# A hybrid HGRN2 and retention layer: bursts ordered by tile shape, copies first in a tree's level, bounds and tables inside the opening

## The chip, the core and the metric

The kernel runs on one core of a Trainium2 chip. The core has a matmul engine (PE, with its weight loads shown as PEld), a vector engine (DVE), a scalar engine (ACT), a general engine (POOL), and SP, whose queue issues most of the DMAs. Each engine takes its own instructions in a fixed order and waits on semaphores for the others. The metric is the device time of one execution in microseconds (us); lower is better.

## The reference

The layer takes x (2048 positions of 1024 features) and a condition c. What is computed, in one pass:

```python
mod = silu(c) @ w_ada + b_ada                   # shift, scale, gate
h = rms_norm(x, norm_g) * (1 + scale) + shift
hq, hf, hi, hz, rq, rk, rv, rz, ga, gb = split(h @ w_in)
f = lb + (1 - lb) * sigmoid(hf); k = 1 - f; q = silu(hq)   # lb from hg_lb_logits, a softmax
S_t = diag(f_t) S_{t-1} + k_t hi_t^T;  oA_t = S_t^T q_t    # HGRN2, 8 heads of 128
oB = retention(rotary(rq), rotary(rk), rv)                 # 8 heads, dk 64, dv 128, causal decay
uA = head_rms_norm(oA) * silu(hz); uB = head_rms_norm(oB) * silu(rz)
m = sigmoid(ga) * uA + sigmoid(gb) * uB
out = rms_norm(x + gate * (m @ w_out), final_g)
```

## The kernel before, in words

**Products.** The projection h @ w_in is done in two halves of 1024 positions. Its columns are cut into "quads" of kinds a (HGRN2 q and f of a head), b (retention q and k), v (the two value streams) and A, B (gates), in the order of the table `ORDER`. Each quad is a 2 by 2 block product done with seven products instead of eight (a Strassen form): product m = 1 to 7 of quad q multiplies a left operand (the parts A11, A12, A22 of h, or the sums S1 to S4 of them) by a right operand (a weight part or a sum of weight parts) and adds into one PSUM bank, tag v, x or y. Every operand is split into a rounded high part and a remainder, and `product_step` issues three 128x512 matmuls for each of the 4 steps along the contraction: 12 matmuls for a product. ACT makes the high part (L295) and DVE the remainder (L296). Product 2 takes A12 (in the trace simply A) and a weight as it is, with no sum on either side; products 5, 3 and 6 take S1 to S4. `product_order` (L55) lists the sequence of (m, quad).

**The end of a product.** `after` (L486) evicts a bank by ACT (L483, `stash`) or adds it by DVE (L496, L503, L507) and hands the block to `deliver`, which starts what follows for it: sigmoid, f, k and q for kind a (`take_a`, L580 to L590), a transposition for v (`take_v`, L597).

**Background.** Everything else is cut into steps that stand between the products. `Background.burst` (L201) is called about every 8 matmul steps and runs one step of each generator in its one list `lanes`. A head's `tree` and `hgrn_out` are appended to that list; a pair's `retention` is put at its front. So a burst's order is retention, then the tree and the output of each head as they were appended. PE takes its instructions in the order in which the program gives them; the order on the other engines is laid out by a scheduler from priorities (`FIRSTS` = 2000, `PEV` = 600, else 0).

**The tree.** For each head and half, the products of decays within a chunk are built in levels m = 1, 2, 4, 8, 16, 32, 64. Level m makes 64 small matmuls (128 deep, 32 or fewer wide; from m = 16 on fewer and larger ones) into a bank of tag lv, of which there is one. Then DVE multiplies q (L787), k (L788), below m = 16 also every 16th column k0 (L791), and f (L792) for the next level, and copies the level's result out of the bank through masks into `ad` (L794 for the diagonal, L799); from m = 16 on ACT copies it into `af` (L812, L818). The next level's matmuls need the new q and k, and the bank.

**HGRN2 output and retention.** A step of `hgrn_out` makes three matmul pairs into poh. A retention step transposes a key block, makes the scores (64 deep, tile rt), adds the cross term from the state rs (64 deep) and scm times v (128 deep) into pos, and the state's update kz times v (64 wide). Both end in `normed` (L833): ACT sums squares (L838), POOL makes the power (L174, L177), ACT scales (L841).

**The opening** (L1108 to L1247) has no sums of h yet. It builds h by 8 feature blocks in the order KO while DVE reduces two weight rows of w_ada for each (L355, read by `ada_load` through SP), and adds quad 0 with plain products into the banks c00, c10, c11 (tag x0) and c01, and products 1 and 2 of quad 1 beside them (x1, y1; c_y in the trace is the tile that holds c01 and y1). Behind its loop stand `lower_bounds` (L159 to L169, an exponential on ACT), the four deliveries of quad 0, `late_consts` and `tables` (L614), which reads the cosine and sine tables, transposes them on DVE (L618) and stores them to DRAM (lin) with 12 DMAs from SP.

## Time and profile before

| what | value |
|---|---|
| time, median of 3 runs | 2061.95 us (2058.75 to 2062.59) |
| time of the profiled execution | 2059.39 us |
| its span from the first to the last instruction | 2057.6 us |
| mean granted clock of PE | 0.988 |
| PE busy | 1950.7 us, 95% of the span |
| DVE, ACT, POOL busy | 1413.2, 984.9, 284.5 us |
| DMA | 126 GB/s on average |

A row of the timeline gives the start and the length of a merged group of equal instructions, its engine and line, out<-in by the program's names, how many, and in brackets how long the engine was idle before it and which instruction ended that. Lengths of matmuls are modelled and overlap the next ones; the distance between two starts is the better measure. 128\*32 is the tile of the array that a matmul takes.

### The profile page before, as it was taken

What the parts mean: (1) busy time and instruction counts of PE and PEld (TensorE: products, weight loads), DVE (VectorE), ACT (ScalarE), POOL (GpSimd) and SP (SyncE); (2) the same over time, 40 slices, a digit from 0 to 9 for tenths busy, and PEclk for the clock granted to TensorE, in tenths of its full rate; (3) what the DMA queues carried; (4) which work ended last, traced back from release to release, by engine and by line L of the source; (5) the groups of instructions that cost most, each with busy time, mean ns of one, the idle gap of its engine ahead of it and who ended that gap; (6) DMA issues with size and microseconds to landing.
All of it is one profiled execution on the core that took longest, in us unless ns stands there. A gap on an engine that the chain in (4) does not pass through costs nothing. (4 is left out here: it accounts for less than half of the span.)

```text
span 2057.6 us, 40131 instructions
## 1 busy us (share of the span) xinstructions
PE 1950.7 (95%) x15172; PEld 1581.2 (77%) x15172; DVE 1413.2 (69%) x2677; ACT 984.9 (48%) x2426; POOL 284.5 (14%) x522
## 2 busy tenths in 40 slices
PE   4889899998999989999999999998999999999998
PEld 3668688877778777777787788877788878787887
DVE  5885767666767767677987676676757675768332
ACT  4634444554555446445544545544454445445331
POOL 2002210121013210201002020211011101110000
PEclk9999999999999999999999999999999999999999
DMA  9144424343353545446544424354434433245542
GB/s 305 43 106 122 129 78 115 101 133 114 113 159 113 138 133 157 144 149 201 153 104 128 121 79 109 100 147 127 115 100 123 122 84 114 69 128 189 160 147 83
DMA packets 453122, 259.97 MB, mean 126 GB/s; under 512 B 171713, under 2 KB 406209, under 8 KB 452929
## 3 DMA queue, kind: packets, MB, share of 16 engines
q1 hardware_dynamic: 286752, 172.89, 29.5%
q10 hardware_dynamic: 153120, 76.04, 13.1%
q0 software_dynamic: 13056, 8.47, 1.6%
q8 instruction: 120, 1.97, 0.4%
q14 instruction: 74, 0.60, 0.1%
HBM read 188.03 MB, written 69.21 MB: 125 GB/s over the span
## 5 line engine op out<-in xcount | busy, mean ns | idle before, releaser
L296 DVE TENSOR_TENSOR b<-w,b 128x512 fp32r<-128x512 f32 (+1 forms) x553 | 346.7, 635 | 312.8 <-ACT b L295 304.0
L71 PE MATMUL v<-S,b 128*128 128x512 f32 x1704 | 430.8, 401 | 10.6 <-ACT S L295 5.0
L295 ACT ACTIVATE b<-w 128x512 fp32r<-128x512 f32 (+1 forms) x553 | 316.8, 583 | 256.1 <-PE x L71 169.3
L71 PE MATMUL x<-S,b 128*128 128x512 f32 x1704 | 433.3, 399 | 5.0 <-DVE c L503 4.4
L71 PE MATMUL x<-A,b 128*128 128x512 f32 x1704 | 424.6, 397 | 3.9 <-ACT c L483 3.0
L71 PEld LDWEIGHTS v<-S,b 128*128 128x128 f32 x1704 | 320.4, 192 | 82.7 <-ACT c L483 7.5
L71 PEld LDWEIGHTS x<-A,b 128*128 128x128 f32 x1704 | 317.6, 190 | 71.1 <-ACT c L483 4.2
L71 PEld LDWEIGHTS x<-S,b 128*128 128x128 f32 x1704 | 312.8, 189 | 67.6 <-ACT uh L838 3.3
L71 PE MATMUL y<-A,b 128*128 128x512 f32 x840 | 207.5, 395 | 1.8 <-DVE ro L650 1.8
L421 DVE TENSOR_TENSOR w<-w,w 128x512 f32<-128x512 f32 x284 | 195.0, 687 | 3.8 <-DMA w<-in_w_d_dram 0.3
L71 PEld LDWEIGHTS y<-A,b 128*128 128x128 f32 x840 | 155.6, 189 | 34.4 <-issue 2.2
L71 PE MATMUL ops<-wo,m 128*128 128x512 f32 x768 | 174.5, 389 | 0.0
L71 PEld LDWEIGHTS ops<-wo,m 128*128 128x128 f32 x768 | 144.1, 188 | 29.9
L174 POOL TENSOR_SCALAR ssh<-ssh 128x1 f32<-128x1 f32 x128 | 49.7, 388 | 788.8 <-ACT uh L838 785.6
L483 ACT ACTIVATE c<-v 128x512 f32<-128x512 f32 x142 | 84.5, 595 | 123.9 <-PE v L71 106.0
L841 ACT ACTIVATE uh<-poh,rrh 128x128 f32<-128x128 f32 x128 | 47.1, 368 | 137.4 <-POOL rrh L177 131.8
L71 PEld LDWEIGHTS lv<-q,k 128*32 128x32 f32 (+1 forms) x5888 | 70.1, 109 | 54.3 <-issue 39.9
L71 PE MATMUL lv<-q,k 128*32 128x16 f32 (+2 forms) x5888 | 81.4, 188 | 29.2 <-DVE ad L799 12.4
L787 DVE TENSOR_TENSOR q<-q,f 128x512 f32<-128x512 f32 x112 | 76.9, 687 | 16.8 <-PE lv L71 16.6
L177 POOL TENSOR_TENSOR rrh<-ssh,mhalf 128x1 f32<-128x1 f32 x128 | 86.3, 674 | 10.4
L503 DVE TENSOR_TENSOR c<-c,x 128x512 f32<-128x512 f32 x71 | 48.8, 687 | 53.5 <-PE x L71 53.3
L176 POOL TENSOR_TENSOR ssr<-ssr,epsx 128x2 f32<-128x2 f32 x64 | 20.5, 321 | 457.2 <-ACT ur L838 457.1
(191 smaller groups left out, 2446.9 us busy)
## 6 DMA issues: line engine op xcount, KB each, us to landing
w<-in_w_d_dram ACTq DMA_DIRECT2D x128, 256.0 KB
w<-in_w_c_dram ACTq DMA_DIRECT2D x66, 256.0 KB
mu<-ud SPq DMA_DIRECT2D x64, 256.0 KB
w<-in_w_a_dram ACTq DMA_DIRECT2D x60, 256.0 KB
wa<-in_w_ada_dram SPq DMA_DIRECT2D x16, 512.0 KB
w<-in_w_b_dram ACTq DMA_DIRECT2D x32, 256.0 KB
vd<-vt SPq DMA_DIRECT2D x128, 64.0 KB
vh<-vd SPq DMA_DIRECT2D x64, 128.0 KB
```

The costliest lines, as they stand in the source:

```text
L71: return tc.keep_in_program_order(nc.tensor.matmul(**kw))
L174: G.tensor_scalar(out=ss, in0=ss, scalar1=n * EPS, scalar2=None, op0=ALU.add)
L176: G.tensor_tensor(out=ss, in0=ss, in1=eps, op=ALU.add)
L177: G.tensor_tensor(out=dst, in0=ss, in1=mhalf.broadcast_to([P, w]), op=ALU.pow)
L295: S.activation(out=t[0], in_=src, func=AF.Copy)
L296: return V.tensor_tensor(out=t[1], in0=src, in1=t[0], op=ALU.subtract)
L421: V.tensor_tensor(out=out, in0=x, in1=y, op=ALU.add)
L483: S.activation(out=t, in_=ps, func=AF.Copy)
L503: V.tensor_tensor(out=t, in0=t, in1=xb[q], op=ALU.subtract)
L787: V.tensor_tensor(out=qv, in0=qv, in1=tv[:, :, :, 0:1].broadcast_to([P, NU, nb, m]), op=ALU.mult)
L841: S.activation(out=dsts[i], in_=pos[i], func=AF.Copy, scale=rr[:, i : i + 1])
```

## The change

1. **Order of products.** Product (2, quad 1) moves from behind (6, 1) to directly behind the opening, ahead of (5, 1), (3, 1) and (6, 1). It takes the bank that held c11, so c11 is delivered second, with priority `FIRSTS` for c11 and c10, and the opening's plain steps fill c11 and its neighbour before c10.
2. **Bounds and tables.** The load of `lg` moves up to second on SP and `lower_bounds` to the start of the opening; `tables` moves from behind the opening into its loop, at step 5 of 10.
3. **Bursts.** `lanes` is parted in three lists; a burst runs HGRN2 outputs, then retentions, then trees.
4. **Retention step.** The matmuls that are 128 deep (the transposition, scm times v) come first, then those 64 deep (cross term, scores), then the 64 wide (kz times v). The cross term closes the sum that it opened before.
5. **Tree level.** The copies out of the bank come ahead of the four multiplications.

```diff
--- before.py
+++ after.py
@@ -53,10 +53,10 @@
 
 
 def product_order():
-    made = [(5, 1), (3, 1), (6, 1)]
+    made = [(2, 2), (5, 1), (3, 1), (6, 1)]
     for i in range(1, NQ):
         n = i + 1
-        made += [(2, n), (7, i), (1, n), (5, n), (4, i), (3, n), (6, n)] if n < NQ else [(7, i), (4, i)]
+        made += [(7, 1), (1, 2), (5, 2), (4, 1), (3, 2), (6, 2)] if i == 1 else [(2, n), (7, i), (1, n), (5, n), (4, i), (3, n), (6, n)] if n < NQ else [(7, i), (4, i)]
     return made
 
 
@@ -140,13 +140,13 @@
         xrows.append(pool.tile([P, n], F32, name=f"xrow{t}", tag=tag, bufs=bufs)[:, 0:1024])
         nc.sync.dma_start(out=xrows[t], in_=a["x"][t * P : (t + 1) * P, :])
 
+    lg = upool.tile([P, 256], F32, name="lg", tag="dT", bufs=1)[:, 0 : 2 * H]
+    nc.sync.dma_start(out=lg, in_=a["lb_t"])
     ng = const("ng", [P, KT], a["ng_t"])
     bad = const("bad", [P, 2 * KT], a["bada_t"])
     for t in range(4):
         load_rows(t)
 
-    lg = upool.tile([P, 256], F32, name="lg", tag="dT", bufs=1)[:, 0 : 2 * H]
-    nc.sync.dma_start(out=lg, in_=a["lb_t"])
     lb = cpool.tile([P, H], F32, name="lb", tag="lb")
     omlb = cpool.tile([P, H], F32, name="omlb", tag="omlb")
     nomlb = cpool.tile([P, H], F32, name="nomlb", tag="nomlb")
@@ -190,6 +190,8 @@
 
         def __init__(self):
             self.lanes = []
+            self.rets = []
+            self.trees = []
             self.side = []
             self.late = []
             self.since = 0.0
@@ -200,14 +202,16 @@
 
         def burst(self):
             done = False
-            now = list(self.lanes)
+            now = self.lanes + self.rets + self.trees
             while now:
                 again = []
                 for g in now:
                     try:
                         said = next(g)
                     except StopIteration:
-                        self.lanes.remove(g)
+                        for z in (self.rets, self.trees, self.lanes):
+                            if g in z:
+                                z.remove(g)
                         done = True
                         continue
                     done = done or said is not True
@@ -258,7 +262,7 @@
 
         def drain(self):
             for _ in range(4000):
-                if not (self.lanes or self.side or self.posts):
+                if not (self.rets or self.trees or self.lanes or self.side or self.posts):
                     return
                 self.force()
             raise RuntimeError("the background does not end")
@@ -589,7 +593,7 @@
         else:
             V.tensor_tensor(out=q[:, tb * 512 : (tb + 1) * 512], in0=z, in1=sg, op=ALU.mult)
         if (ch, tb) == (0, 1):
-            bg.lanes.append(tree(h, sb, f, k, q))
+            bg.trees.append(tree(h, sb, f, k, q))
             bg.lanes.append(hgrn_out(h, sb))
 
     def take_v(sb, h, s, tb, z):
@@ -607,7 +611,7 @@
 
         bg.post(5.0, store)
         if (s, tb) == (0, 1) and h % 2:
-            bg.lanes.insert(0, retention(h // 2, sb))
+            bg.rets.insert(0, retention(h // 2, sb))
 
     lin = dram("lin", [3, 32, L])
 
@@ -784,12 +788,6 @@
             qv = q.rearrange("p (j n two m) -> p j n two m", j=NU, two=2, m=m)[:, :, :, 1, :]
             kv = kk if m >= 16 else k[:, 1 : NU * 512 + 1]
             kv = kv.rearrange("p (j n two m) -> p j n two m", j=NU, two=2, m=m)[:, :, :, 0, :]
-            V.tensor_tensor(out=qv, in0=qv, in1=tv[:, :, :, 0:1].broadcast_to([P, NU, nb, m]), op=ALU.mult)
-            V.tensor_tensor(out=kv, in0=kv, in1=tv[:, :, :, 1:2].broadcast_to([P, NU, nb, m]), op=ALU.mult)
-            if m < 16:
-                k0 = k16j[:, :, :, 0]
-                V.tensor_tensor(out=k0, in0=k0, in1=t_cur.rearrange("p j (n t) -> p j n t", n=32)[:, :, :, 1], op=ALU.mult)
-            V.tensor_tensor(out=f[:, :, 0:nb], in0=tv[:, :, :, 0], in1=tv[:, :, :, 1], op=ALU.mult)
             if m == 1:
                 V.copy_predicated(
                     out=ad.rearrange("p c (w j) -> p c w j", w=2)[:, :, :, 0], mask=dmsk,
@@ -813,6 +811,12 @@
                         out=af[r0 : r0 + m, :, r0 + m : r0 + 2 * m],
                         in_=ps[r0 : r0 + m, 0 : NC * m].rearrange("p (c t) -> p c t", t=m), func=AF.Copy,
                     )
+            V.tensor_tensor(out=qv, in0=qv, in1=tv[:, :, :, 0:1].broadcast_to([P, NU, nb, m]), op=ALU.mult)
+            V.tensor_tensor(out=kv, in0=kv, in1=tv[:, :, :, 1:2].broadcast_to([P, NU, nb, m]), op=ALU.mult)
+            if m < 16:
+                k0 = k16j[:, :, :, 0]
+                V.tensor_tensor(out=k0, in0=k0, in1=t_cur.rearrange("p j (n t) -> p j n t", n=32)[:, :, :, 1], op=ALU.mult)
+            V.tensor_tensor(out=f[:, :, 0:nb], in0=tv[:, :, :, 0], in1=tv[:, :, :, 1], op=ALU.mult)
             if m == 8:
                 for r0 in range(0, P, 32):
                     S.activation(out=af[r0 : r0 + 32, :, r0 : r0 + 32], in_=ad[r0 : r0 + 32], func=AF.Copy)
@@ -978,23 +982,25 @@
             if n < CH:
                 kz = po[:, P : 2 * P]
                 PE.transpose(out=kz, in_=qks[n][:, 1, :], identity=ident)
+            if n:
+                vb_ = [vrs[m][:, j, :] for j in range(2)]
+                pos = [po[:, 0:P], pt[:, 1, P : 2 * P]]
+                for j in range(2):
+                    PE.matmul(
+                        out=pos[j], lhsT=scms[m][:, j], rhs=vb_[j], start=True, stop=g == 0, skip_group_check=True
+                    )
+                if g:
+                    for j, r in enumerate(rows):
+                        PE.matmul(
+                            out=pos[j], lhsT=qks[m][r, 0, :], rhs=rs[r, :], start=False, stop=True, skip_group_check=True
+                        )
+            if n < CH:
                 for j, r in enumerate(rows):
                     PE.matmul(out=pt[:, j, 0:P], lhsT=qks[n][r, 1, :], rhs=qks[n][r, 0, :], start=True, stop=True)
             if n:
-                vb_ = [vrs[m][:, j, :] for j in range(2)]
-                pos = [po[:, 0:P], pt[:, 1, P : 2 * P]]
-                if g:
-                    for j, r in enumerate(rows):
-                        PE.matmul(
-                            out=pos[j], lhsT=qks[m][r, 0, :], rhs=rs[r, :], start=True, stop=False, skip_group_check=True
-                        )
                 if not last:
                     for j, r in enumerate(rows):
                         PE.matmul(out=x[r, :], lhsT=kzs[m][:, r], rhs=vb_[j], start=True, stop=True)
-                for j in range(2):
-                    PE.matmul(
-                        out=pos[j], lhsT=scms[m][:, j], rhs=vb_[j], start=g == 0, stop=True, skip_group_check=True
-                    )
             if n < CH:
                 scms[n] = upool.tile([P, 2, P], F32, name=f"scm{p}_{g0 + n}", tag="scm", bufs=1)
                 V.tensor_tensor(out=scms[n], in0=pt[:, :, 0:P], in1=dT.rearrange("p (j t) -> p j t", j=2), op=ALU.mult)
@@ -1106,6 +1112,8 @@
 
 
     def opening():
+        with tc.high_priority(offset=FIRSTS):
+            lower_bounds()
         diag = [upool.tile([P, 512], F32, name=f"diag{i}", tag="mu", bufs=4) for i in range(2)]
         with tc.high_priority(offset=FIRSTS):
             scb = row_of_c()
@@ -1209,6 +1217,8 @@
             if s < 2:
                 for t in (4 + 2 * s, 5 + 2 * s):
                     stats(t)
+            if s == 5:
+                tables()
             if s + 2 < KT:
                 was[KO[s + 2]] = ada_load(KO[s + 2])
             if s + 1 < KT:
@@ -1223,7 +1233,7 @@
                 product_step(yb[1] if m == 2 else xb[1], m, 1, j, j == 0, j == 3)
             if s >= 2:
                 kt = KO[s - 2]
-                for ch in range(2):
+                for ch in (1, 0):
                     plain_step(acc[ch, 1], 2 * (kt // 4) + ch, ats[1, kt], kt)
                 if kt >= 4:
                     j = kt - 4
@@ -1231,13 +1241,11 @@
         for m in (1, 2):
             W.parts.pop((m, 1))
         after(2, 1)
-        lower_bounds()
-        with tc.high_priority(offset=PEV):
-            for ch, tb in ((0, 0), (1, 0), (1, 1), (0, 1)):
+        for ch, tb in ((0, 0), (1, 1), (1, 0), (0, 1)):
+            with tc.high_priority(offset=FIRSTS if ch else PEV):
                 deliver(0, ch, tb, acc[ch, tb])
         after(1, 1)
         late_consts()
-        tables()
 
     opening()
     af = upool.tile([P, NC, P], F32, name="af", tag="af", bufs=1)
```

Where instructions move, as the program's order on each engine shows it:

**PE behind the opening.** The last plain matmuls of the opening, and the first products. A_0_3 is a split block of h; S_ are sums; c, c_y the opening's banks, y, v, x those of products, lv the tree's. Before:

```order
L71 MATMUL c_346<-A_0_3_721,bp_1_317 128x512
L71 MATMUL v_818<-S_0_0_519,b_1_819 128x512 x3
...
L71 MATMUL v_818<-S_0_3_749,b_1_823 128x512 x3
L71 MATMUL x_347<-S_0_0_527,b_1_826 128x512 x3
...
L71 MATMUL y_904<-A_0_0_373,b_2_850 128x512 x3
...
L71 MATMUL lv_0_1_922<-q_0_766,k_0_765 32x16 x32
```

and with the change:

```order
L71 MATMUL c_y_353<-A_0_3_752,bp_321 128x512 x3
L71 MATMUL y_823<-A_0_0_383,b_2_824 128x512 x3
...
L71 MATMUL v_850<-S_0_0_529,b_1_829 128x512 x3
...
L71 MATMUL v_850<-S_0_3_780,b_1_833 128x512 x3
L71 MATMUL x_357<-S_0_0_537,b_1_851 128x512 x3
...
L71 MATMUL lv_0_1_925<-q_0_787,k_0_786 32x16 x32
```

On ACT, the split of the same last block of h (A_0_3), before and with the change:

```order
L1142 ACTIVATE h_1_7_719<-xps_7_714,mods 128x512
L295 ACTIVATE b_1_819<-w_0_324 128x512
L580 ACTIVATE sg_0_0_0_768<-c_344 128x512
L295 ACTIVATE b_1_823<-w_3_328 128x512
L295 ACTIVATE S_0_2_711<-h_2_487 128x512
L295 ACTIVATE A_0_3_721<-h_1_7_719 128x512
L164 ACT_TABLE_LOAD
```

```order
L1150 ACTIVATE h_1_7_750<-xps_7_745,mods 128x512
L584 ACT_TABLE_LOAD
L584 ACTIVATE sg_0_0_0_789<-c_354 128x512
L299 ACTIVATE b_2_824<-w_2_334 128x4x64
L586 ACTIVATE f_0_785<-sg_0_0_0_789,lb,omlb 128x512
L589 ACTIVATE k_0_786<-sg_0_0_0_789,omlb,nomlb 128x512
L299 ACTIVATE b_1_829<-w_0_336 128x512
L299 ACTIVATE b_2_824<-w_2_334 128x4x64
L299 ACTIVATE S_0_2_742<-h_2_497 128x512
L299 ACTIVATE A_0_3_752<-h_1_7_750 128x512
```

The y product now stands first, and the split of A_0_3, for which the opening's last plain matmuls wait, stands behind a table load, f, k and a sigmoid, of which only a sigmoid stood ahead of it.

**SP in the second half of the opening.** The last w_ada rows and the tables. Before, then with the change:

```order
L332 DMA wa_0_534<-in_w_ada_dram 128x1024
L332 DMA wa_1_536<-in_w_ada_dram 128x1024
L332 DMA wa_0_575<-in_w_ada_dram 128x1024
L332 DMA wa_1_577<-in_w_ada_dram 128x1024
L944 DMA dT_0_1653<-in_dT_dram 128x256
```

```order
L621 DMA tab_585<-in_cos_dram 128x512
L336 DMA wa_0_544<-in_w_ada_dram 128x1024
L336 DMA wa_1_546<-in_w_ada_dram 128x1024
L628 DMA lin<-tabt_586 512x1x32 x4
L621 DMA tab_593<-in_sin_dram 128x512
L336 DMA wa_0_606<-in_w_ada_dram 128x1024
L336 DMA wa_1_608<-in_w_ada_dram 128x1024
L628 DMA lin<-tabt_594 512x1x32 x4
```

The last pair of w_ada rows now stands behind four stores of the transposed cosine table, which wait for DVE.

**DVE in the first tree's first level.** Between the level's matmuls and the next level's. Before, then with the change:

```order
L788 TENSOR_TENSOR k_0_765<-k_0_765,f_0_764 128x512
...
L296 TENSOR_TENSOR b_2_1059<-w_3_834,b_2_1059 128x4x64 x2
L791 TENSOR_TENSOR k_0_765<-k_0_765,f_0_764 128x64
L794 COPY_PREDICATED ad<-dmsk,lv_0_1_922 128x16
L792 TENSOR_TENSOR f_0_764<-f_0_764 128x2x256
L799 COPY_PREDICATED ad<-msk,lv_0_1_922 128x128
```

```order
L792 COPY_PREDICATED ad<-dmsk,lv_0_1_925 128x16
L425 TENSOR_TENSOR w_0_351<-w_0_351,w_3_859 128x512
L797 COPY_PREDICATED ad<-msk,lv_0_1_925 128x128
L425 TENSOR_TENSOR w_2_334<-w_2_334,w_0_351 128x512
L814 TENSOR_TENSOR q_0_787<-q_0_787,f_0_785 128x512
L815 TENSOR_TENSOR k_0_786<-k_0_786,f_0_785 128x512
...
L818 TENSOR_TENSOR k_0_786<-k_0_786,f_0_785 128x64
L601 STREAM_TRANSPOSE vt_0_0_0_969<-c_1_902 128x512
L819 TENSOR_TENSOR f_0_785<-f_0_785 128x2x256
```

The copy that empties the bank came last of the level and now comes ahead of its multiplications. The line numbers of the changed kernel run 2 to 8 higher or, for the copies, 2 lower, as the diff shifts them.

## The prediction

> **What bounds the kernel now.** I read the busy time by stages first (columns: the stretch, its length, then busy time and number of instructions of PE, PEld, DVE, ACT and POOL, granted clock, DMA share, GB/s).
>
> ```profile
> 0.00:102.00 102.00, 67.01 (x300) 51.72 (x300) 70.30 (x142) 56.40 (x94) 16.69 (x35) 0.97 0.54 174
> 102.00:152.00 50.00, 41.12 (x506) 32.42 (x505) 40.84 (x78) 15.47 (x35) 3.31 (x5) 0.93 0.48 105
> 152.00:1900.00 1748.00, 1692.30 (x13706) 1372.98 (x13707) 1244.38 (x2362) 868.84 (x2205) 252.35 (x452) 0.99 0.44 124
> ```
>
> PE is the bound: behind 152 us it is 97% busy. What can be won lies in its waits: 35 us idle in the first stage and 9 us, at a clock of 0.93, in the second. The change removes no matmul. So I read PE's timeline from the end of the opening through the first tree, where the releaser in brackets names each wait.
>
> ```profile
> 79.08 0.50 PE L71 MATMUL c_y<-A,bp 128*128 128x512 f32 x1 [2.07 <-ACT A L295]
> 80.33 1.08 PE L71 MATMUL c_y<-A,bp 128*128 128x512 f32 x2 [0.75 <-DVE A L296]
> 81.20 1.49 PE L71 MATMUL c<-A,bp 128*128 128x512 f32 x3
> 82.48 3.61 PE L71 MATMUL v<-S,b 128*128 128x512 f32 x12
> 86.78 2.35 PE L71 MATMUL v<-S,b 128*128 128x512 f32 x9 [0.69 <-ACT c L483]
> 94.11 2.03 PE L71 MATMUL v<-S,b 128*128 128x512 f32 x3 [4.99 <-ACT S L295]
> 95.94 3.71 PE L71 MATMUL x<-S,b 128*128 128x512 f32 x12
> 99.48 2.89 PE L71 MATMUL y<-A,b 128*128 128x512 f32 x12
> 102.38 0.72 PE L71 MATMUL lv<-q,k 128*32 128x16 f32 x64
> ...
> 111.66 1.05 PE L71 MATMUL lv<-q,k 128*32 128x16 f32 x64 [2.88 <-DVE ad L799]
> 112.64 3.94 PE L71 MATMUL v<-S,b 128*128 128x512 f32 x12
> ...
> 135.09 0.73 PE L71 MATMUL lv<-q,k 128*16 128x16 f32 x64 [3.08 <-DVE f L792]
> 135.75 4.32 PE L71 MATMUL x<-A,b 128*128 128x512 f32 x12
> ...
> 152.02 1.00 PE L71 MATMUL lv<-q,k 128*64 128x64 f32 x16 [2.94 <-DVE k L788]
> ```
>
> A wait costs more than its length. An undisturbed product, as at 99.48, shows 2.89, the one behind 2.88 us of idleness 3.94, that behind 3.08 us 4.32: 1.1 to 1.4 us more, at the lowered clock of that stage. [...]
>
> **The opening and the first products.** Product 2 needs only A12 and a raw weight, both there, so 12 matmuls (2.72 to 2.9 us) can run ahead of the wait of 4.99 us for the last sums, and of the 0.69. Moving work into a wait should gain up to that wait. Against it stand two new delays. First, the last pair of w_ada rows, which ran without a gap on SP, now stands behind the cosine stores.
>
> ```profile
> L332 SPq DMA_DIRECT2D wa<-in_w_ada_dram x16: 328/430/4092, 13.2 to 42.5; - x16
> 56.73 1.29 DVE L296 TENSOR_TENSOR S<-h,S 128x512 fp32r<-128x512 f32 x2
> 64.04 1.28 DVE L355 CUSTOM_DVE_ANT_0 wa<-wa,scb,bad 128x1024 f32<-128x1024 f32 x1
> 95.52 2.68 SPq L624 DMA_DIRECT2D lin<-tabt  x4
> 111.08 2.85 SPq L624 DMA_DIRECT2D lin<-tab  x4
> 117.44 0.65 POOL L637 DMA_DIRECT2D sn<-lin  x1 [1.92 <-DMA lin<-tab]
> ```
>
> The transposition for those stores comes between the two S of 56.73, so it is done near 58; four issues take 2.68 us, and the rows are asked for near 61.5 instead of 42.5. DVE reduced the second of them from 64.04. With some 4 us from issue to data (my estimate, from the 3.5 us between the end of the four issues of 111.08, at 113.93, and the sine load at 117.44 that waits for what they store), the reductions end near 68 instead of 65.3: 2.5 us late, and with them the last blocks of h, for which PE waits. If the stores and their 128-byte pieces clog the queue it may be 6; if the scheduler's other work fills in, 1.
>
> Second, ACT's row ahead of the split of the last block of h.
>
> ```profile
> 77.89 0.62 ACT L295 ACTIVATE S<-h 128x512 fp32r<-128x512 f32 x1
> 78.41 0.62 ACT L295 ACTIVATE A<-h 128x512 fp32r<-128x512 f32 x1
> 79.04 1.28 ACT L164 ACT_TABLE_LOAD   x1
> 88.53 0.80 ACT L582 ACTIVATE f<-sg,lb,omlb 128x512 f32<-128x512 f32 x1
> ```
>
> Before, b, sg, b and S stood there, about 0.52 each. Now it is a table load (1.28), sg (0.5), f and k (0.71 each, start to start), b in three pieces (1.1) and S (0.52): 4.8 instead of 2.1, so 2.7 us later; the wait of 2.07 grows to about 4.8. In return the table loads at 79.04 and, later, for the return to the sigmoid become one, and the bounds no longer stand in the way; ACT has slack for that, so I count nothing. [...]
>
> So PE reaches the end of the opening at 82.48 + 2.5 + 2.7 = 87.7. From there product 2, two v and one x take 4 x 2.72 = 10.9, about 0.8 of wait for the first S and 0.7 of slow clock stay, and the tree's first level starts near 100 instead of 102.38: **2 us gained** (from 5 lost to 5 gained).
>
> **The first tree.** From 102.38 to 152.02 PE waits 2.88 + 3.08 + 2.94 = 8.9 us for DVE, and the slow products behind add 1.05 + 1.43 + about 1.3 = 3.8. The first wait is for the copy L799 behind all of the level's multiplications; with the change the copies stand ahead of them, the bank is free early, and the q, k and k0 that the next level needs come without f in between. I take that wait as gone: 2.88 + 1.05 = 3.9. Below 16 wide the waits for f and k at 135.09 and 152.02 come from DVE being full (40.84 of 50 us); the tables' transpositions and copies are out of this stage (0.7 of DVE, and the stores' slots), and the order of DVE shows f and the rotations further apart. I take two thirds of 3.08 + 2.94 + 2.7, less 2 us for a wait that comes back at the levels 32 and 64: about 4. Together **8** (4 to 10).
>
> **The later trees.** The same wait comes at seven other trees. The row groups level matmuls by their shape; the rows below are one case.
>
> ```profile
> L71 PE MATMUL lv<-q,k 128*32 128x16 f32 x4096 | 47.2, 185 | 12.4 <-DVE ad L799 12.4
> 1021.89 0.28 DVE L791 TENSOR_TENSOR k<-k,f 128x64 f32<-128x64 f32 x1
> 1025.81 0.43 DVE L799 COPY_PREDICATED ad<-msk,lv 128x128 f32<-128x128 uint8 x1
> 1026.38 0.72 PE L71 MATMUL lv<-q,k 128*32 128x16 f32 x64 [1.83 <-DVE ad L799]
> ```
>
> Of 12.4 us, 2.88 belong to the first tree, so 9.5 remain. In the case shown k0 was done at 1022.2, four us before the copy; with the copy first, PE would find its operands before it arrives at 1024.55. But two copies (0.2 and 0.3 on DVE) now stand ahead of q, k, k0, and f comes later for the level after. I take 80%: **7.5** (4 to 9.5).
>
> **The bursts.** The count of tile shape changes in PE's order falls from 424 to 388, all at bursts in which a tree's 128\*32 matmuls now stand behind the 64-wide ones. What a change costs shows in one burst:
>
> ```profile
> 184.22 0.49 PE L71 MATMUL poh<-vh,k 128*128 128x128 f32 x2
> 184.55 0.39 PE L71 MATMUL poh<-vh,af 128*128 128x128 f32 x2
> 184.77 0.39 PE L71 MATMUL poh<-st,q 128*128 128x128 f32 x2
> ```
>
> Two matmuls behind a change start the next pair 0.33 later, two without one 0.22: 0.1 a change. 36 x 0.09 to 0.11 gives **3.3** (0 if the changes hide elsewhere, 4).
>
> The order of bursts does more: HGRN2's pair now comes before retention's, so ACT, which serves both normalisations, meets them in the other order. Its waits for POOL's power are long already:
>
> ```profile
> ACT uh L841 <- POOL rrh L177: 131.8, 122, 4.2
> 883.14 0.37 ACT L841 ACTIVATE uh<-poh,rrh 128x128 f32<-128x128 f32 x1 [1.65 <-POOL rrh L177]
> 884.04 0.66 PE L74 MATMUL uT<-ident,mu 128*128 128x128 f32 x4 [1.48 <-ACT c L483]
> ```
>
> They cost PE where an eviction L483 stands behind, as at 884.04. In ACT's order retention's two scalings now mostly follow its squares with nothing between, where before HGRN2's squares filled about half of them. I expect ACT to wait some 1 us more in each of half the 64 retention bursts; but ACT is busy only half of the time behind 152 us, and the evictions have a product (2.72 us) of time. **Nothing**, between 5 gained (the rs chain on DVE runs earlier) and 8 lost.
>
> **The sum.** 2 + 8 + 7.5 + 3.3 = 20.8. The profiled execution took 2059.39, so 2038.6; the median of the three runs is 2.6 above that execution, and I give 2041.
>
> **Rivals.** *B, the opening and first tree give it back.* w_ada's rows land 6 us late, or the waits of the first tree move to other levels, since DVE has the same work there. For it: DVE's 40.84 of 50 us; against it: the first wait is one of order, not of work. Then 3.3 + 5 or 6 remain: 2051. *C, ACT blocked on POOL.* If each of 64 retention bursts holds up an eviction long enough to cost PE 0.35 to 0.7 us more, that is 22 to 45 us, against 20.8 gained: 2060 to 2085, slower from 0.4 us a burst on. For it: 884.04 shows the path; against it: ACT is idle half of the time, so a late scaling is soon made up, and 884.04 is one of the longer waits of its kind. *D, the change does not do what it says.* Shape changes cost nothing when weights load anyway, and the copies wait for PE's level instead of the multiplications, so DVE stands still and everything behind it is late: within 4 us of 2060.
>
> **The numbers.** The forecast has 0.66, B 0.15, C 0.10, D 0.09. A difference of 0.2%, 4 us, is about what a measurement of this kernel can tell from none. Faster: 0.66 + 0.13 from B and less from the tails, 0.77; same: 0.12, from D and the edge of B and C; slower: 0.11. The range is 2027 (all upper bounds: 5 + 10 + 9.5 + 4 + 5 is 33) to 2059, where B and part of D lie; the likeliest case alone spans 2030 to 2050.
>
> **What would show it.** Right: the first tree level starts near 100 us and the level-64 one near 142; the row of the lv group loses most of its 12.4; the wait of 4.99 is gone and one of about 4.8 stands at the last A split. Wrong: PE's c matmuls wait over 6 us near 70, new lv waits of 2 us and more at other levels, or a larger total of waits for c L483.

## The result, and the profile after

The changed kernel takes 2047.98 us (median of 4 runs, 2047.56 to 2048.44), the kernel before 2061.36 us beside it. The ratio is 0.9937, with a 95% interval of 0.992 to 0.9954: 13 us or 0.63% faster. The forecast was 2041, in a range of 2027 to 2059: the direction was right and the gain too large, 20.8 us against 13.4.

Where it came from shows when the profiled span (2057.6 us before, 2046.1 after) is cut at two marks of the first tree. In the timeline of PE of the changed kernel (start, length, what, and in brackets the wait before it and what ended it):

```profile
83.30 2.14 PE L71 MATMUL c<-A,bp 128*128 128x512 f32 x3 [4.95 <-ACT A L299]
85.23 1.48 PE L71 MATMUL c_y<-A,bp 128*128 128x512 f32 x3
86.85 3.79 PE L71 MATMUL y<-A,b 128*128 128x512 f32 x12
...
99.79 0.72 PE L71 MATMUL lv<-q,k 128*32 128x16 f32 x64
106.27 5.49 PE L71 MATMUL x<-S,b 128*128 128x512 f32 x12 [5.77 <-DVE c L507]
...
149.16 0.69 PE L71 MATMUL lv<-q,k 128*64 128x64 f32 x16 [2.34 <-DVE k L815]
```

| stretch | before | after | gained | forecast |
|---|---|---|---|---|
| start to the first tree's level 1 | 102.38 | 99.79 | 2.6 | 2 |
| level 1 to level 64 | 49.64 | 49.37 | 0.3 | 8 |
| level 64 to the end of the span | 1905.6 | 1896.9 | 8.7 | 10.8 (7.5 + 3.3) |

The first and the last stretch came out within about 2 us of the forecast. The first tree gave nothing, though of its three waits before (2.88, 3.08 and 2.94 us) only the last is left, at 2.34: a wait of 5.77 us that no rival had named stands behind its first level, and the product behind it takes 5.49 us where an undisturbed one shows 2.88: the granted clock was 0.50 over it (106.27 to 111.50). DVE of the changed kernel shows what is late there:

```profile
104.93 0.69 DVE L425 TENSOR_TENSOR w<-w,w 128x512 f32<-128x512 f32 x1 [5.41 <-DMA w<-in_w_b_dram]
105.54 0.68 DVE L507 TENSOR_TENSOR c<-c,x 128x512 f32<-128x512 f32 x1
```

L425 is a sum of two raw weights of quad 2, and it waits for one of them from DRAM. L507, which takes product (6,1) out of the bank that the next product needs, is ready at about 99.7, but stands behind it. ACT issues those two loads (ACTq rows), first in the kernel before and then in the changed one:

```profile
79.10 0.61 ACTq L406 DMA_DIRECT2D w<-in_w_b_dram  x1
83.44 0.61 ACTq L406 DMA_DIRECT2D w<-in_w_b_dram  x1
```

```profile
91.13 0.64 ACTq L410 DMA_DIRECT2D w<-in_w_b_dram  x1
94.44 0.61 ACTq L410 DMA_DIRECT2D w<-in_w_b_dram  x1
```

They go out 11 to 12 us later. The second is used 10.5 us after its issue, with DVE waiting. So the first theory was: the product that was moved to the front takes one of the three split buffers first, the split for (6,1) must wait for that product's end, and only that split frees the raw weights' places that the two loads need. (The moved product is number 2 of quad 2, (2, 2) in the diff; the part on the change above calls its quad 1, which is a slip.)

### The profile page after: what moved, and what is told of

Same layout as the page of the kernel before. It is cut to its first block, busy times and chain, and to the rows that moved or that the text cites. A ratio compares the mean times of both kernels' runs of the same rounds, so it can differ in the third digit from the quotient of the medians.

```text
span 2046.1 us, 40140 instructions
## 1 busy us (share of the span) xinstructions
PE 1942.0 (95%) x15172; PEld 1587.0 (78%) x15172; DVE 1417.0 (69%) x2677; ACT 981.2 (48%) x2426; POOL 281.7 (14%) x522
## 4 chain that ended last, share of the span: by engine, by line
PE 61%; DVE 8%; DMA 7%; ACT 7%; POOL 4%; issue 3%; ACTq 1%; SPq 0%; POOLq 0%; DVEq 0%
PE x L71 25%; PE v L71 12%; PE ops L71 9%; PE y L71 6%; PE lv L71 3%; PE poh L71 2%; DVE b L300 2%; ACT b L299 2%; POOL rrh L177 1%; PE uT L74 1%; PE rt L71 1%; DVE w L425 1%; DMA wg<-in_w_gate_dram 1%; PE por L71 1%; POOL rrr L177 1%
## 5 line engine op out<-in xcount | busy, mean ns | idle before, releaser
L71 PE MATMUL v<-S,b 128*128 128x512 f32 x1704 | 425.6, 398 | 4.2 <-ACT c L487 4.0
L425 DVE TENSOR_TENSOR w<-w,w 128x512 f32<-128x512 f32 x284 | 194.8, 686 | 10.6 <-DMA w<-in_w_b_dram 5.4
L487 ACT ACTIVATE c<-v 128x512 f32<-128x512 f32 x142 | 84.6, 596 | 121.4 <-PE v L71 97.8
L177 POOL TENSOR_TENSOR rrh<-ssh,mhalf 128x1 f32<-128x1 f32 x128 | 88.7, 693 | 10.5
L507 DVE TENSOR_TENSOR c<-c,x 128x512 f32<-128x512 f32 x71 | 48.7, 685 | 51.7 <-PE x L71 51.5
L815 DVE TENSOR_TENSOR k<-k,f 128x512 f32<-128x512 f32 x112 | 76.8, 686 | 0.0
```

The source lines that it names most:

```text
L71: return tc.keep_in_program_order(nc.tensor.matmul(**kw))
L177: G.tensor_tensor(out=dst, in0=ss, in1=mhalf.broadcast_to([P, w]), op=ALU.pow)
L425: V.tensor_tensor(out=out, in0=x, in1=y, op=ALU.add)
L487: S.activation(out=t, in_=ps, func=AF.Copy)
L507: V.tensor_tensor(out=t, in0=t, in1=xb[q], op=ALU.subtract)
L815: V.tensor_tensor(out=kv, in0=kv, in1=tv[:, :, :, 1:2].broadcast_to([P, NU, nb, m]), op=ALU.mult)
```

## The experiments

Each run is compared with the kernel before on its own chip, in six runs and more of each (five in two cases). A ratio's interval is about 0.003 wide, so two runs on different chips that differ by less than 4 us are not told apart by their times; the traces then decide.

**The order of products undone.** All else of the change stays.

```diff
-    made = [(2, 2), (5, 1), (3, 1), (6, 1)]
+    made = [(5, 1), (3, 1), (6, 1)]
...
-                for ch in (1, 0):
+                for ch in range(2):
...
-        for ch, tb in ((0, 0), (1, 1), (1, 0), (0, 1)):
-            with tc.high_priority(offset=FIRSTS if ch else PEV):
+        with tc.high_priority(offset=PEV):
+            for ch, tb in ((0, 0), (1, 0), (1, 1), (0, 1)):
```

> The changed kernel with the order of products, of deliveries and of the opening's plain steps as before; bursts, copies, bounds and tables stay changed. Theory (the product put first takes a split buffer, so the split for product (6,1) and with it the loads of the next quad's weights come some 11 us later, and a sum of weights on DVE waits for them with the eviction behind it): the wait of 5.77 us for c L507 at 106 us is gone, the first tree takes 41 us from its first level to level 64 instead of 49.4, the wait of about 5 us for the last sums S is back, and the whole takes 2041 to 2045 us. Rival (DVE is simply full in the first tree, and the wait would come at another place): the first tree still takes 47 to 50 us, and with the S wait back the whole takes 2050 to 2053 us.

Measured: 2042.6 us, 0.9917 (0.99 to 0.9933). PE's timeline of this run:

```profile
84.60 0.79 PE L71 MATMUL c_y<-A,bp 128*128 128x512 f32 x1 [5.34 <-ACT A L299]
...
92.68 3.19 PE L71 MATMUL v<-S,b 128*128 128x512 f32 x12 [0.69 <-ACT c L487]
...
101.34 0.72 PE L71 MATMUL lv<-q,k 128*32 128x16 f32 x64
...
142.29 0.69 PE L71 MATMUL lv<-q,k 128*64 128x64 f32 x16 [2.34 <-DVE k L815]
```

The tree takes 40.95 us, and the wait for L507 is gone: theory, not rival. But half of the expectation failed. The wait of 5 us for the last sums S is not back, although the product that was to fill it stands in its old place again. So it was not product 2 that removed that wait; the bounds did, as a run below shows. With product 2 in front the first level starts at 99.79 instead of 101.34, but 1.0 of these 1.5 us is there from the first matmul on (11.70 against 12.66), and kernels with one and the same opening differ by more: the kernel before and the next two runs on it have 102.38, 102.94 and 104.50. So what product 2 alone is worth is not shown.

**A split buffer of its own.** The changed kernel, and the first product's weight is split into the place of `af`, which lies free until the opening ends.

```diff
-        W.pump(i + NBW)
+        W.pump(i + NBW + (i == 2))
...
+        W.split(halves(upool.tile([P, 2, 512], F32R, name="b2_2", tag="af", bufs=1)))
```

> The changed kernel, but the split of the first product's weight goes into a buffer of its own (the place of af, free until the opening ends) instead of a turn of the ring of three. Theory: the split for (6,1) no longer waits for that product's end, the two weight loads go out at about 83 and 92 us instead of 91.13 and 94.44, and the wait at 106 us shrinks from 5.77 to 0 to 3 us: 2040 to 2045 us. Rival (DVE full): the two loads come earlier but DVE has no less to do, 2047 to 2049 us.

Measured: 2042.82 us, 0.9913 (0.9898 to 0.9928). First ACT's queue, then PE:

```profile
80.73 0.61 ACTq L410 DMA_DIRECT2D w<-in_w_b_dram  x1
90.62 0.63 ACTq L410 DMA_DIRECT2D w<-in_w_b_dram  x1
```

```profile
99.73 0.72 PE L71 MATMUL lv<-q,k 128*32 128x16 f32 x64
100.93 3.00 PE L71 MATMUL x<-S,b 128*128 128x512 f32 x12 [0.48 <-DVE c L507]
...
140.92 1.12 PE L71 MATMUL lv<-q,k 128*64 128x64 f32 x16 [2.34 <-DVE k L815]
```

The loads go out at 80.73 and 90.62, the wait shrinks to 0.48 us, and level 64 comes at 140.92 instead of 149.16, 8.2 us earlier. With the run above this settles the lost gain of the first tree: it was a place in a buffer ring, not DVE's load.

**The copies alone,** on the kernel before (the block of the four multiplications moves below the copies, as in the diff of the change).

```diff
-            V.tensor_tensor(out=qv, in0=qv, in1=tv[:, :, :, 0:1].broadcast_to([P, NU, nb, m]), op=ALU.mult)
...
             if m == 1:
                 V.copy_predicated(
...
+            V.tensor_tensor(out=qv, in0=qv, in1=tv[:, :, :, 0:1].broadcast_to([P, NU, nb, m]), op=ALU.mult)
...
```

> The kernel before with the copies ahead of the multiplications and nothing else. Theory: the waits of the level matmuls for ad (12.4 us) fall to some 2, and the slow matmuls behind the first go too: 11 us less, 2050 us; the waits at 135 and 152 us stay. Rival (the wait only moves, since q, k and k0 come later by the two copies): 2056 us or more.

Measured: 2052.37 us, 0.996 (0.9945 to 0.9975). PE's timeline and its group row:

```profile
102.94 0.72 PE L71 MATMUL lv<-q,k 128*32 128x16 f32 x64
111.45 0.73 PE L71 MATMUL lv<-q,k 128*32 128x16 f32 x64 [2.06 <-DVE k L814]
...
152.64 0.85 PE L71 MATMUL lv<-q,k 128*64 128x64 f32 x16 [2.96 <-DVE k L811]
```

```profile
L71 PE MATMUL lv<-q,k 128*32 128x16 f32 x4096 | 46.9, 185 | 5.7 <-DVE k L814 5.7
```

The group's waits fall from 12.4 to 5.7, and 8 us of time are gained (5 to 11 by the interval). In the first tree alone nothing is gained: 49.70 us, where 49.64 stood. There the wait for the copy only becomes one for k0, as the rival said. In the seven later trees 9.5 becomes 3.6. But the profiled execution, one of the slower of the six, shows only 4.3 us less of span, and the sum of all of PE's waits behind the first tree fell there by only 1.9 us (54.9 to 53.0, counted as in the table below), since others grew: the one for the retention's keys (por) from 4.5 to 6.5. So how 5.9 us less of waiting for the tree becomes 8 us of time is not shown.

**The bursts alone,** on the kernel before: three lists, and the retention step's new order.

```diff
-            now = list(self.lanes)
+            now = self.lanes + self.rets + self.trees
...
```

> The kernel before with the bursts' order and the retention step's order of the change and nothing else. Theory: 36 fewer shape changes at 0.09 us give 3.3 us, the waits around ACT's and POOL's norms even out to 0 to 2 us more: 2058 to 2060 us. Rival 1 (shape changes cost nothing in the stream of weight loads): 2061 us or more. Rival 2 (ACT held by POOL's power): 2065 us and more, with a larger sum of PE waits for c L483.

Measured: 2061.33 us, 1.0004 (0.999 to 1.0017): no difference. That is the time of rival 1, but not its reason. To see why I took, from the first level-64 matmul to the end, the distances between starts of consecutive matmuls, and parted them into those behind matmuls of 128x512, those behind the small ones, and the waits over 0.15 us.

| kernel | shape changes there | small matmuls, us | 128x512, us | waits, us | clock of that profile |
|---|---|---|---|---|---|
| before | 411 | 306.0 | 1537.0 | 54.9 | 0.988 |
| bursts alone | 375 | 300.0 | 1542.1 | 56.8 | 0.980 |
| the change | 375 | 298.8 | 1534.4 | 56.0 | 0.987 |

The small matmuls gain 6 to 7 us, twice my 3.3. Waits take 2 back, and the large matmuls 5, at a lower clock.

What the clock did stands in the traces of these runs. In them the granted clock is recorded as 1.0 or 0.5, and it changed only at multiples of 3.41 us: in steps, as I call them. In the fourteen profiles (without the first 20 and the last 15 us of each), every step at 1.0 in which PE stood idle for 2.0 us or more, 99 of them, was followed by a step at 0.5, and none with less than 1.2 us of idleness was; between the two it went both ways, 41 times out of 216. From the first level-64 matmul on the profiles have 6 to 13 steps at 0.5, and the large matmuls take some 1.4 us more for each (1530.9 us with 6, 1542.1 with 13; a straight line through the fourteen misses them by 0.7 us, as a standard deviation). The kernel before has 9 there, the bursts alone 13. Whether the bursts' order makes such steps, or its waits only fall otherwise on these steps, stays open: there are 6 to 9 in the four profiles with 411 shape changes and 6 to 13 in the nine with 375, and over all runs of this comparison the mean clock is 0.9843 with the bursts changed and 0.9866 before.

**The tables late again,** on the run with the old order of products.

```diff
-            if s == 5:
-                tables()
...
         late_consts()
+        tables()
```

> As the run with the old order of products (2042.6 us), but the tables are read and stored behind the opening again, as before; the bounds stay early. Theory A (the 8.7 us that the first tree lost between the copies alone and that run come from the tables: late tables put rotations and sums of weights close together on DVE ahead of the tree's multiplications): the first tree takes 47 to 50 us again instead of 41, with waits of 2 us and more for k at the levels 2, 16 and 64; 2048 to 2052 us. Theory B (they come from the bounds, by f and k being there earlier): the first tree stays at 41 us, 2041 to 2044 us.

Measured: 2051.12 us, 0.9956 (0.9939 to 0.9973). Theory A. First PE, then DVE and POOL of this run:

```profile
98.83 0.72 PE L71 MATMUL lv<-q,k 128*32 128x16 f32 x64
...
107.32 0.73 PE L71 MATMUL lv<-q,k 128*32 128x16 f32 x64 [2.09 <-DVE k L818]
...
131.41 0.69 PE L71 MATMUL lv<-q,k 128*16 128x16 f32 x64 [3.42 <-DVE k L818]
...
150.28 1.12 PE L71 MATMUL lv<-q,k 128*64 128x64 f32 x16 [4.64 <-DVE k L815]
```

```profile
111.51 0.66 POOL L641 DMA_DIRECT2D sn<-lin  x1 [10.81 <-DMA lin<-tabt]
118.12 0.69 DVE L652 TENSOR_TENSOR sw<-c,sn 64x512 f32<-64x512 f32 x1
...
131.00 0.27 DVE L818 TENSOR_TENSOR k<-k,f 128x64 f32<-128x64 f32 x1
...
149.45 0.68 DVE L815 TENSOR_TENSOR k<-k,f 128x512 f32<-128x512 f32 x1
```

and the same two steps with the tables early (the run with the old order of products):

```profile
94.33 1.33 POOL L641 DMA_DIRECT2D sn<-lin  x2
111.25 0.69 DVE L652 TENSOR_TENSOR sw<-c,sn 64x512 f32<-64x512 f32 x1
```

With late tables POOL asks for the sine rows 17 us later, and the first rotation of a retention block starts at 118 instead of 111. The rest of that rotation (L653 to L655, until 127.9) stands on DVE ahead of the k that level 16 waits for; the later rotations stand, with little between them, from 138 to 148, ahead of the k for level 64, which waits 4.64 us instead of 2.34. At level 2 a table's transposition (L622, at 104.46) is one of four operations between k and k0, where early tables leave one. The tree takes 51.45 us instead of 40.95. On the other side the first level starts at 98.83 instead of 101.34 (0.5 us of it from an earlier first matmul): early tables cost the opening about 2.5 us, as forecast, and give the tree 10.5.

**The bounds late again,** on the same run.

```diff
-        with tc.high_priority(offset=FIRSTS):
-            lower_bounds()
...
         after(2, 1)
+        lower_bounds()
```

> As the run with the old order of products (2042.6 us), but the bounds and the load of their table stand behind the opening again, as before; the tables stay early. Theory A: the first tree stays near 41 us, and the wait of about 5 us for the last sums S is back, since the exponential's table load and f and k stand ahead of those sums on ACT again, while the wait of 5.3 us for the last split of A falls to about 2: 2041 to 2046 us. Theory B: the first tree is back at 47 to 50 us, 2048 us or more.

Measured: 2044.7 us, 0.9927 (0.9911 to 0.9942). PE, then ACT:

```profile
78.83 0.49 PE L71 MATMUL c_y<-A,bp 128*128 128x512 f32 x1 [1.14 <-ACT A L299]
...
91.02 4.86 PE L71 MATMUL v<-S,b 128*128 128x512 f32 x12 [4.90 <-ACT c L487]
```

```profile
84.68 1.28 ACT L164 ACT_TABLE_LOAD   x1
85.97 0.21 ACT L164 ACTIVATE lbt<-lbt 128x16 f32<-128x16 f32 x1
86.21 1.28 ACT L584 ACT_TABLE_LOAD   x1
```

The wait of 5 us changes places: with early bounds it stands at the last split of A, with late ones behind two table loads, sigmoids, f and k, where the next eviction (L487, at 90.36 on ACT) is held up. The first level starts at 101.33 against 101.34, the tree takes 40.93. So moving the bounds is worth nothing here; it is the tables that count.

**Both delays of the opening taken out.** On the kernel with its own split buffer: tables at step 6, behind the last w_ada rows, and a sigmoid of one column right behind the exponential at the start, so that no table load stands near the last split.

```diff
-            if s == 5:
+            if s == 6:
                 tables()
+        S.activation(out=lg[:, 0:1], in_=lg[:, 0:1], func=AF.Sigmoid)
```

> The changed kernel with the own split buffer (2042.8 us), and beside it the tables one step later in the opening, behind the last w_ada rows on SP, and a sigmoid of one column right behind the exponential, so that the sigmoid's table load stands at the start. Theory (the two delays of the opening that the prediction named): the wait of 2.13 us near 67 us falls below 0.5, the wait of 4.90 us for the last split of A falls to 2 to 3, the first tree level starts 3 to 5 us earlier, 2037 to 2040 us. Rival (the last rows of h come no earlier, since DVE is the limit of the opening): 2041 to 2043 us.

Measured: 2046.39 us, 0.9935 (0.9919 to 0.995), above what theory and rival expected. From 2042.82 without the two edits, on another chip, the time alone does not tell it apart: the intervals overlap. PE and ACT:

```profile
71.10 2.08 PE L71 MATMUL xps<-diag,xrow 128*128 128x128 f32 x8 [4.85 <-ACT h L1151]
...
79.95 0.50 PE L71 MATMUL c<-A,bp 128*128 128x512 f32 x1 [0.50 <-ACT A L300]
...
100.42 4.61 PE L71 MATMUL x<-S,b 128*128 128x512 f32 x12 [4.11 <-DVE c L508]
```

```profile
70.27 0.78 ACT L1151 ACTIVATE h<-xps,mods 128x512 f32<-128x512 f32 x1 [0.66 <-DMA lin<-tabt]
```

The two waits fell (near 67 none is left, 4.90 became 0.50), and the first level started at 95.59, 4.1 us earlier. But at 70 us PE now waits 4.85 us for a block of h, which ACT makes behind its copy of a table (L626, at 68.47) and a wait of 0.66 us for the tables' stores; its matmuls start at 71.10, 0.7 us later than without the two edits (70.39), so this block comes no earlier, as the rival said. And the weight loads, whose place on ACT's queue moved with the splits (87.57 and 90.13), are late again: 4.11 us for L508, the same instruction as L507 before, under a shifted number. Level 64 comes at 142.04 instead of 140.92.

**Bursts undone on the kernel with its own buffer.**

```diff
-            now = self.lanes + self.rets + self.trees
+            now = list(self.lanes)
...
```

and the old retention step.

> The changed kernel with the own split buffer (2042.8 us), with the order of bursts and of the retention step as before. Theory (fewer shape changes save 6 us of matmul time, and the early scm products wait some 4 us for ACT's scaling, with more waits for c L483 beside them): small matmuls take 306 us instead of 300 behind the first tree, the waits for ur at rt are gone, and the whole takes 2041 to 2045 us, no difference that can be told. Rival (the 6 us are a gain in full): 2047 to 2050 us.

Measured: 2043.16 us, 0.9917 (0.9901 to 0.9933), against 2042.82 with them: no difference again. The theory's numbers hold: small matmuls take 307.5 us instead of 300.4, and scm times v no longer waits for ur. Its reason holds less well. The waits in all did not shrink (56.7 us against 54.1, since por now waits 7.0 us, for the keys' load and for ur, instead of 3.8); the large matmuls took 1530.9 us instead of 1537.7. As with the bursts alone, what the small matmuls lose or win comes back in the large ones: behind the first tree this profile has 6 steps at a clock of 0.5, the other 11.

**Only the early sigmoid,** once with the old order of products and once with the own buffer.

```diff
...
+        S.activation(out=lg[:, 0:1], in_=lg[:, 0:1], func=AF.Sigmoid)
...
```

> As the run with the old order of products (2042.6 us), with a sigmoid of one column right behind the exponential at the start, so that no table load stands ahead of the last split of A on ACT. Theory: the wait of 5.34 us for that split falls by the 1.28 us of the load, to about 4.0, and the first tree level starts some 1.3 us earlier; 2041 us. [...]

> The changed kernel with the own split buffer (2042.8 us) and the early sigmoid. Theory: the wait for the last split of A falls from 4.90 to about 3.6, but the wait for c L507 behind the tree's first level grows from 0.48 by up to the same 1.3 us, because the second weight load goes out behind the split for (6,1) and takes its time: 2042 to 2043 us, no gain. Rival (that load moves along with the opening): 2041 us and c L507 stays at 0.5.

Measured: 2039.63 us, 0.9903 (0.9884 to 0.9922), and 2038.1 us, 0.9897 (0.9878 to 0.9916). The wait for the last split falls from 5.34 to 3.92 and from 4.90 to 3.47, by one table load of 1.28 and little else. But the first level starts at 97.36 and 96.83, some 4 and 3 us earlier, more than that load. (Of the 3 us a part may be scatter: three more kernels here with the own buffer and the same opening have 97.89, 97.98 and 100.00 where the first has 99.73.) PE of the second run, and of the kernel with its own buffer for comparison:

```profile
8.72 3.78 PE L71 MATMUL scp<-dgs,ones 128*128 128x512 f32 x4 [8.72 <-DVE dgs L347]
...
80.16 2.03 PE L71 MATMUL c<-A,bp 128*128 128x512 f32 x3 [3.47 <-ACT A L300]
...
98.03 2.32 PE L71 MATMUL x<-S,b 128*128 128x512 f32 x9 [0.47 <-DVE c L508]
```

```profile
12.07 3.78 PE L71 MATMUL scp<-dgs,ones 128*128 128x512 f32 x4 [12.07 <-DVE dgs L346]
```

The whole opening starts 3.4 us earlier, and this is no scatter: the first matmuls stand at 8.4 to 8.8 us in the three runs with the early sigmoid and at 11.1 to 14.6 in all others. With the extra table load in ACT's order at the start, the scheduler no longer puts a split, which waits for ACT, ahead of dgs on DVE (dgs starts at 7.47 and 7.80 in the two runs; in the change a split stands at 10.03 and dgs at 10.64), and PE's first matmuls need dgs. My expectation for the second run, no gain since the weight load would be late again, was wrong: L508 waits 0.47 us. This median is the lowest here, next to one of 2038.29 below from which it is not told apart; its interval lies below that of the change.

**One half of the bursts' change each,** on the kernel with its own buffer: first the old retention step with the new lists, then the new step with the old lists.

```diff
...
-                        out=pos[j], lhsT=scms[m][:, j], rhs=vb_[j], start=True, stop=g == 0, skip_group_check=True
+                        out=pos[j], lhsT=scms[m][:, j], rhs=vb_[j], start=g == 0, stop=True, skip_group_check=True
...
```

```diff
-            now = self.lanes + self.rets + self.trees
+            now = list(self.lanes)
...
```

> The changed kernel with the own split buffer (2042.8 us), with the retention step's order as before and the bursts' order as changed: 424 shape changes in PE's order, as before, instead of 388. If a change costs 0.17 us (6.2 us for 36 in the traces so far), small matmuls behind the first tree take 306 to 307 us instead of 300, and the waits of rt for ur are gone; 2042 to 2046 us. If the time of small matmuls hangs on which matmuls stand together and not on the count, they take 300 to 303.

> The changed kernel with the own split buffer (2042.8 us), with the bursts' order as before and the retention step's order as changed: 406 shape changes in PE's order. By 0.17 us a change, small matmuls behind the first tree take 303 us; the waits of rt for ur, since scm times v still stands first, stay near 4 us; 2042 to 2046 us.

Measured: 2040.88 us, 0.9911 (0.9897 to 0.9926), and 2038.29 us, 0.9897 (0.9881 to 0.9914). Of the 36 shape changes that the whole takes away, the new lists alone take none and the new step alone 18. Behind the first tree small matmuls take 305.2 us with 411 changes and 302.1 with 393; the kernel before has 306.0 with 411, the own buffer 300.4 with 375. So their time follows the count of shape changes, at 0.18 us each (the mean of the four profiles with 411 changes is 306.2, of the nine with 375 it is 299.6, and 6.6 / 36 = 0.18). The waits of scm times v for ur are 0 in the first, as expected, and 1.4 us in the second, not 4; there por waits 9.3 us in its place. Both times lie below what I expected, and they do not follow the count: with neither half, either or both the ratios are 0.9917, 0.9911, 0.9897 and 0.9913, and all four intervals overlap.

## Why the prediction was right in direction and too large

**The opening, 2 us.** Measured 2.6, and the two new delays were nearly as priced: the last A split waited 4.95 us (4.8 forecast), product 2 started at 86.85 (87.7), the first level at 99.79 (near 100). The sum hides two errors that cancel, and with the scatter of about 2 us between kernels of one opening its nearness is in part luck. The wait of 4.99 us, which I gave to product 2 to fill, is removed by the bounds, whose price is the longer wait at the split of A: with the old order of products it is gone too. And the opening began 2.2 us earlier, since the first matmuls start at 11.70 instead of 13.86, which I had not looked for. The price of a table load, 1.28 us in the row at 79.04 (ACT's next row starts 1.30 behind it), held nearly too: taking one load out of the way shortened the wait by 1.42 and 1.43 us in two runs.

**The first tree, 8 us: the step that failed.** Two things. "Product 2 needs only A12 and a raw weight, both there" priced the operands of the moved product and not what it holds while it runs: a split buffer, and through it the split for (6,1) and two weight loads. That is 5.77 us of wait and 2.6 us of slow matmuls behind it. And the reason for the gain was another one than I gave. The copies alone gain nothing in this tree; with the copies in place the early tables do, whose own instructions on DVE I had counted as 0.7 us. What moves is when the sine rows arrive and so where the rotations stand. (Whether early tables would do as much with the copies behind the multiplications, no run shows.) Nor was DVE full, as I had read its 40.84 of 50 us: from level 1 to level 64 it is busy for 40.5 of 49.64 us before and for 39.6 of 41.19 with the own buffer, so its work stayed and its idle time went. With the buffer freed, the tree takes 41.2 us and gains 8.5: the size was right by luck, for a wrong reason and behind a wait that I had missed. The change alone reaches level 64 at 149.16, and my sign for being right was near 142. The 12 matmuls behind the wait of 5.77 us took 5.49 us at a granted clock of 0.50. But waits of 2.34 us were followed by 4.61 us for the next 12 matmuls in this profile and by 3.02 with the old order of products, so the wait's length alone does not set the tail. What differs between these two is where the wait falls on the steps of 3.41 us. The rows show three steps around each of these two waits, first of the change, then of that run (stretch, length, PE busy, granted clock, DMA share, GB/s):

```profile
146.57:149.99 3.42, 1.08 (x19) 1.00 0.29 74
149.99:153.40 3.41, 3.41 (x9) 0.50 0.42 94
153.40:156.81 3.41, 3.41 (x16) 1.00 0.44 96
```

```profile
138.07:141.48 3.41, 1.87 (x9) 1.00 0.35 110
141.48:144.89 3.41, 2.60 (x25) 1.00 0.44 88
144.89:148.31 3.42, 3.42 (x17) 1.00 0.62 138
```

In the change the whole wait lies in one step, which leaves PE 1.08 us of work, and the next step runs at a clock of 0.50; in the other run the steps part it into 1.5 and 0.8 us, and the clock stays at 1.00.

**The later trees, 7.5 us.** Right for the wait, not shown for the time. The group's waits without the first tree fall from 9.5 to 2.5 us:

```profile
L71 PE MATMUL lv<-q,k 128*32 128x16 f32 x4096 | 47.3, 185 | 2.5 <-DVE k L818 2.5
```

But the sum of PE's waits behind the first tree did not fall with it: 54.9 us before, 56.0 with the change, and 56.7 with the bursts as before and the own buffer, where v's waits grew from 4.6 to 8.5 and por's from 4.5 to 6.9. The 8.7 us that the last stretch gained are, by the table of the bursts, 7.2 of small matmuls and 2.6 of large ones, less 1.1 of waits. So it is in part luck that this stretch came out near the forecast, which expected 7.5 of waits and 3.3 of small matmuls.

**The bursts, 3.3 us, and ACT, nothing.** A shape change came to 0.18 us here (6.6 us for 36) and not to 0.09 to 0.11; my row showed only the matmul behind the change, and the rest may lie ahead of it. So small matmuls gained 7 us. "Nothing" for ACT holds for the sum and not for the places. Two groups wait longer for it; the first row is of the kernel before, where the other group had 0.0, and the next two are of the change:

```profile
L74 PE MATMUL uT<-ident,mu 128*128 128x128 f32 x256 | 39.7, 277 | 10.2 <-ACT c L483 7.9 <-DVE sz L694 2.2
```

```profile
L71 PE MATMUL rt<-vr,scm 128*128 128x128 f32 x128 | 25.3, 280 | 4.5 <-ACT ur L845 4.5
L74 PE MATMUL uT<-ident,mu 128*128 128x128 f32 x256 | 39.7, 278 | 16.3 <-ACT c L487 12.3 <-DVE sz L698 3.9
```

The wait at rt was not foreseen in its place: scm times v now comes early in the step, into a bank from which ACT still reads the step before. That at uT is the path of rival C, evictions behind ACT's scalings, at about 6 us instead of its 22 to 45. The last sign of being wrong that the prediction names came true with it: PE's waits for such evictions (c L483, now L487) grew from 15.4 to 19.0 us. But other waits fell. By the bursts' order all waits behind the first tree grew by 1.9 us on the kernel before and fell by 2.6 with the own buffer (56.7 to 54.1).

**The rivals.** B (the opening and the first tree give it back) named the right stretch, and the measured 2047.98 us lies nearer to its 2051 than to my 2041 (and to 2053, which it is with the 2.6 us that the forecast adds for the median); but the opening kept its gain, and the wait that came is not one of the tree's levels and not of DVE's load. D fits the time of the bursts alone and not the rest.

## What to carry to other kernels

Work that is moved into a wait must be asked what it holds, not only what it needs: here one place in a ring of three buffers delayed two loads by 11 to 12 us, and PE paid for it 20 us behind the moved product, by way of DVE. A gain that a profile shows at one instruction may hang on data that arrive elsewhere; undoing one part at a time showed that the first tree needs the early tables, which were priced as a cost, and that the copies, priced as its gain, give it nothing alone. Time taken out of a full engine's stream (7 us of shape changes) is no gain until the whole is shown to be shorter. And waits of one length did not cost the same here: behind one of 2.34 us the next 12 matmuls took 4.61 us in one kernel and 3.02 in another.

## What was not expected

A sigmoid of one column at the start brought the first level of the tree 2.9 us forward (99.73 to 96.83) with the own buffer and 4.0 with the old order of products. Of this, 1.4 us is the shorter wait for the last split of A; the rest goes with an order of DVE in which the first matmuls' operand stands more than 3 us earlier. The medians are 5 and 3 us lower, which the intervals do not tell apart. The mean granted clock lies between 0.980 and 0.993 in these profiles, and the 128x512 matmuls behind the first tree take between 1531 and 1542 us, more of a difference than the bursts' change makes. In the fourteen profiles it follows the number of 3.41 us steps at a clock of 0.5 (some 1.4 us for each), and wherever the clock fell from 1.0 to 0.5 (ends left out as above), PE had stood idle for 1.2 us or more of the step before; why one kernel has 6 such steps and another 13 is open.
